# One early load on another queue, other orders of units, and one accumulator bank read by ScalarE instead of VectorE, in a hybrid attention and SwiGLU block

## The chip, the cores and the metric

The kernel runs on one core of one Trainium2 chip. The metric is device time in microseconds. A core has TensorE (PE in the profile; its weight loads are PEld), VectorE (DVE), ScalarE (ACT), GpSimd (POOL) and SyncE (SP). They run apart from each other, each in the order of its own instructions, and wait on semaphores. Weights come from HBM by DMA. In this kernel transfers are issued from SP, which only issues, and from POOL.

## The reference, cut to what matters

One layer on 256 rows of 2048 numbers, all in float32:

```
xn   = rms_norm(x, norm1_g)
proj = xn @ w_in                     # q, k, v and two convolution halves: 5120 columns
mix  = [differential attention ; causal convolution, layer norm, silu]
h    = x + mix @ w_out
hn   = rms_norm(h, norm2_g)
y    = h + (silu(hn @ w_gate) * (hn @ w_up)) @ w_down       # hidden width 5632
```

The change lies in the last line. It is the largest part of the work: w_gate, w_up and w_down are 138 MB of the 197 MB of weights.

## The kernel before, in words

**Precision.** Each float32 operand is split into a rounded part (`hi`) and a rest (`lo`), and a product is three matmuls: hi·hi, lo·hi and hi·lo. ScalarE rounds a weight tile (`whi`, line 334; for pairs `wh`, lines 1028 and 1029). VectorE subtracts to get the rest (`wlo`, line 343; for pairs `wl`, lines 1033 and 1034).

**Units.** The work is a list of chunks, `chunks`, in the order in which TensorE multiplies them. In the feed-forward part a chunk is one letter of an order string:

- `g` or `u`, a *two*: two 128-row weight tiles of one matrix, 512 columns wide, times both halves of the rows; 12 matmuls (lines 1068, 1069 and 1073) and a load of 512 KB. In `fast_block`, `g` stands for the second of a pass's two column blocks (w_gate, or the right block of w_down) and `u` for the first.
- a capital `G` or `U`: the same two, but its rest is made without VectorE. ScalarE writes the negated rounded tile into `wlo` (line 337), and a DMA from POOL's queue adds the raw weights to it (line 338).
- `s`, a *pair*: a product of 2 by 2 blocks (two row halves, two 128-row tiles, two column blocks) with seven products instead of eight, 21 matmuls (lines 1050 to 1052). VectorE makes the sums of weight tiles (`pair_sums`, lines 1022 to 1024). A pair loads 1 MB (`load_pair`, line 1015).

**Passes.** A pass is one order string with its eight accumulator banks, Q1 to Q5, Q6, Q7 and QX. The weights' hidden width is cut into blocks j = 0 to 10 of 512 columns. Block 0 is multiplied plainly (`silu_done`, `up_done`), while `make_forms` prepares the row operand for pairs. Block 1 uses `FIRST`, blocks 2 to 10 `ORDER`. After blocks 3, 7 and 10 come two passes each of w_down, with the orders in `DOWN`. That makes 16 passes with pairs.

**End of a pass.** When the last pair of a pass has been multiplied, `bank_sums` combines the banks on VectorE: line 1148 copies Q1 into `w1`, and lines 1149 to 1154 add Q6, Q7, Q5, Q5, Q2 and Q4 in that order. The twos after the last pair use only Q3 and QX, which `block_done` (line 1168) or `down_done` (line 1202) adds when the pass is over. The next pass takes its banks as they are given back. There are four in the pool `acc` (for Q1, Q6, Q7, Q5) and four in `aux` (for Q2, Q4, Q3, QX, and the transposes `ps_a`, line 891). A pair asks for its banks in the order of `PRODUCTS`: Q6, Q7, Q5, Q1, Q2, Q4, Q3.

**Order.** The schedule is written out by hand: `run_chunks` emits, ahead of each chunk's matmuls, the splits of chunks up to 3 further on, the rounding up to 4, the tiles made by DMA and the sums of pairs up to 5, and the loads up to 9. Code that follows a pass runs as generators, moved on by `resume()` inside the chunks. Raw tiles have four buffers, and SP issues loads in program order: a load that must wait holds up all later loads.

**The early load.** The first pair's weights are loaded by `make_forms`, which calls `load_pair` as soon as the memory pool of the earlier stages is closed. They lie in a tile `wb0` in that memory. SP issues this load.

Of the kernel before, what the change touches and what calls it, by code (L numbers as in the profile page):

```python
# [13 lines left out]
F32 = mybir.dt.float32  # L14
# [5 lines left out]
P = 128  # L20
# [12 lines left out]
N = 512  # L33
# [43 lines left out]

ORDER = "sgGsgGsUUsUu"

FIRST = "gugusgsUsGsU"  # L80

Q1, Q6, Q7, Q5, Q2, Q4, Q3, QX = range(8)

PRODUCTS = ((Q6, 5, 1), (Q7, 6, 2), (Q5, 4, 3), (Q1, 0, 5), (Q2, 1, 6), (Q4, 2, 0), (Q3, 3, 4))

DOWN = (dict(pairs=((1, 0), (1, 1), (2, 0)), order=("gsGgsGgsuUuUu",) * 2),
        dict(pairs=((4, 0), (4, 1), (5, 0)), order=("gsGgsGgsuUuUu",) * 2),
        dict(pairs=((8, 0), (8, 1), (9, 0)), order=("sgsGgsuUu",) * 2))

LOAD_AHEAD, DMA_AHEAD, SUMS_AHEAD, HI_AHEAD, LO_AHEAD = 9, 5, 5, 4, 3  # L90

# [17 lines left out]
def tile_block(  # L109
# [6 lines left out]
    act, dve, pool, pe, sp = nc.scalar, nc.vector, nc.gpsimd, nc.tensor, nc.sync  # L116
# [131 lines left out]
    def start(gen):  # L248
        running.append(gen)

    def resume():
        for g in list(running):
            if next(g, StopIteration) is StopIteration:
                running.remove(g)
# [58 lines left out]
    def weights(parts):  # L313

        n = sum(w for _, _, _, w in parts)
        src = wts[next_weight[0] : next_weight[0] + P * n].rearrange("(p n) -> p n", n=n)
        placed_at.append((next_weight[0], n, parts))
        next_weight[0] += P * n
        return src
# [536 lines left out]
    ffn = {}  # L856
# [39 lines left out]
    def place(g):  # L896

        pairs = DOWN[g]["pairs"]
        at = 7 * len(pairs)
# [53 lines left out]
    def make_forms():  # L953
        fp = ffn["pool"]
        load_pair(chunks[pair_at[0]])
        rep = fp.tile([P, S], F32, tag="sum1", name="rep")
        for m in range(NM):
# [49 lines left out]
    def load_pair(c):  # L1007
        if "b" in c:
            return
        if c is chunks[pair_at[0]]:  # L1010
            c["b"] = ffn["pool"].tile([P, 7, N], F32, tag="wl", name="wb0", bufs=2)[:, :4]
        else:
            c["b"] = early.tile([P, 4, N], F32, tag="wb", name="wb")
        src = weights([(w, k, col, N) for w, col in c["sides"] for k in c["ks"]])
        sp.dma_start(out=c["b"].rearrange("p k n -> p (k n)"), in_=src)

    def pair_sums(c):

# [17 lines left out]
    def sum_bank(c, i):  # L1036
        sums = c["sums"]
        if i not in sums:
            tag, pool_ = ("acc", acc_ps) if i < 4 else ("aux", aux_ps)
            sums[i] = pool_.tile([P, N], F32, tag=tag, name=f"q{i}")  # L1040
        return sums[i]

    def multiply_pair(c):
        while not c["ready"](c):
            resume()
        (fhi, flo), p = c["forms"](), c["p"]
        for n, (q, f, w) in enumerate(PRODUCTS):
            ps = sum_bank(c, q)
            first, last = c["first"].get(q), c["last"].get(q)
            pe.matmul(ps, fhi[:, f, p, :], c["hi"][:, w], start=bool(first), stop=False)  # L1050
            pe.matmul(ps, flo[:, f, p, :], c["hi"][:, w], start=False, stop=False)  # L1051
            pe.matmul(ps, fhi[:, f, p, :], c["lo"][:, w], start=False, stop=bool(last))  # L1052
            if n in (1, 3, 5):
                resume()
        resume()
        if c["done"]:
            start(c["done"](c["sums"]))
# [38 lines left out]
    def fast_block(order, side_u, side_g, pairs, twos, **kw):  # L1096

        units, sums = [], {}
        left = dict(s=list(pairs), g=list(twos), u=list(twos))
        for unit in order:  # L1100
            kind = unit.lower()
            p, ks = left[kind].pop(0)
            c = dict(kind=kind, sums=sums, done=None, first={}, last={}, p=p, ks=ks, by_dma=unit.isupper(), **kw)
            if kind == "s":
                c.update(sides=(side_u, side_g), load=load_pair, round=round_pair, split=split_pair,
                         multiply=multiply_pair, uses=[q for q, _, _ in PRODUCTS])
            else:
                w, col = side_g if kind == "g" else side_u
                c.update(w=w, nk=2, width=N, cols=[(col, N)], load=load_chunk, round=round_chunk, split=split_chunk,
                         multiply=multiply_two, uses=(Q3, QX) if kind == "u" else (Q2, Q4))  # L1110
            units.append(c)
        assert not any(left.values())
        for q in range(8):
            users = [c for c in units if q in c["uses"]]
            users[0]["first"][q] = users[-1]["last"][q] = True
        chunks.extend(units)
        return units

    def gate_up_block(j, order):
        units = fast_block(order, ("w_up", j * N), ("w_gate", j * N), [(k, (k, k + HK)) for k in range(NS)],  # L1120
                           [(None, ks) for ks in TWOS], ready=lambda c: "hi" in forms,
                           forms=lambda: (forms["hi"], forms["lo"]),
                           plain=lambda c: [forms["plain"][k] for k in c["ks"]])
        [c for c in units if c["kind"] == "s"][-1]["done"] = products_done
        units[-1].update(done=lambda sums: block_done(j, sums), prompt=True)

    def down_block(g, n):

        last = g == len(FGROUPS) - 1 and n == D // N - 2
        ks = lambda jt: (jt[0] * (N // P) + 2 * jt[1], jt[0] * (N // P) + 2 * jt[1] + 1)  # L1130
        pairs = DOWN[g]["pairs"]
        twos = [(j, t) for j in range(sum(FGROUPS[:g]), sum(FGROUPS[: g + 1])) for t in range(2) if (j, t) not in pairs]
        units = fast_block(DOWN[g]["order"][n // 2], ("w_down", n * N), ("w_down", (n + 1) * N),
                           [(q, ks(jt)) for q, jt in enumerate(pairs)], [(jt, ks(jt)) for jt in twos],
# [7 lines left out]
    halfway = {}  # L1142

    def bank_sums(q):

        fp = ffn["pool"]
        w1, u2, u3, w4 = (fp.tile([P, N], F32, tag=f"sum{i}", name=f"sum{i}") for i in range(4))
        dve.tensor_copy(w1, q[Q1])  # L1148
        dve.tensor_tensor(u2, q[Q6], w1, ALU.add)
        dve.tensor_tensor(u3, q[Q7], u2, ALU.add)  # L1150
        dve.tensor_tensor(w4, q[Q5], u3, ALU.add)
        dve.tensor_tensor(u2, q[Q5], u2, ALU.add)
        dve.tensor_tensor(w1, q[Q2], w1, ALU.add)
        dve.tensor_tensor(u3, q[Q4], u3, ALU.add)
        halfway.update(g=(w1, u3), u=(u2, w4))

    def products_done(q):
        bank_sums(q)
        for t in halfway["g"]:
            act.activation(t, t, AF.Silu)  # L1160
        yield
# [15 lines left out]
    def down_products(n, q, last):  # L1177
        so_far = None
        if last:
            so_far = ffn["pool"].tile([P, 4, N], F32, tag="wt", name="so_far")[:, :NM]  # L1180
            pool.dma_start(out=so_far, in_=out[:, n * N : (n + 1) * N].rearrange("(m p) n -> p m n", p=P))
        bank_sums(q)
        for m in range(NM):
            add_to_out(m, n + 1, halfway["g"][m])
        yield
        if last:
            for m in range(NM):
                dve.tensor_tensor(halfway["u"][m], halfway["u"][m], so_far[:, m], ALU.add)
        halfway["added"] = True
# [43 lines left out]
    for g, nb in enumerate(FGROUPS):  # L1233
        for j in range(j0, j0 + nb):
            if j:
                gate_up_block(j, FIRST if j == 1 else ORDER)
                continue
# [47 lines left out]
```

## Time and profile before

| | |
|---|---|
| median of 3 runs | 1070.22 us (1069.56 to 1076.16) |
| the profiled execution's own time | 1070.12 us |
| its span, first to last instruction | 1068.3 us |
| granted TensorE clock, mean | 0.997 |
| busy: TensorE, VectorE, ScalarE, GpSimd | 1043.2, 899.5, 653.4, 130.7 us |
| moved by DMA | 245.47 MB, 230 GB/s on average |

A row of the timeline has the start in us from the beginning of the span, the duration, engine, line, operation, the tile written and those read, and in brackets the idle time of the engine before it and what ended that. A row of the waits has who waited for whom, then the total in us, how often, and the longest. A row of the groups has how many instructions, then busy time in us and mean ns of one. A TensorE row's duration overlaps its neighbours, so the pace of matmuls is read from one start to the next. A row of the windows has the busy time and number of instructions of PE, PEld, DVE, ACT and POOL, then the granted clock, the share of time in which the DMA engines were busy, and GB/s.

### The profile page before, as it was taken

How to read it: one execution, taken by the hardware profiler on the slowest of the kernel's cores; microseconds unless marked ns; L12 is line 12 of the kernel's file. 1: busy time of each engine (PE TensorE's matmuls, PEld its weight loads, DVE VectorE, ACT ScalarE, POOL GpSimd, SP SyncE). 2: the span in 40 equal slices, each digit the busy share in tenths (PEclk: the TensorE clock that was granted, in tenths of full speed). 3: DMA queues.
4: the chain of work that ended last, by engine and by line, in shares of the span. 5: the costliest groups of instructions: out<-in, count | busy, mean ns of one | idle time of the engine just before them, and what ended most of it. 6: DMA issues, size and time to landing. Idle time of an engine off the chain costs nothing.

```text
span 1068.3 us, 13248 instructions
## 1 busy us (share of the span) xinstructions
PE 1043.2 (98%) x4780; PEld 860.2 (81%) x4780; DVE 899.5 (84%) x1124; ACT 653.4 (61%) x831; POOL 130.7 (12%) x176
## 2 busy tenths in 40 slices
PE   8999999999999899899999999999999999999998
PEld 7888888877888787687878888878878888888776
DVE  4799988899666389989887789899987897989994
ACT  6544566756656466575665565765764656658551
POOL 0120112200100100010102120100101121001011
PEclk9999999999999999999999999999999999999999
DMA  8656555444446466986969998969878999889774
GB/s 300 206 180 200 189 183 173 158 158 158 158 158 242 171 196 223 291 240 222 320 165 319 269 289 283 290 206 330 235 239 247 262 307 330 239 249 263 242 214 89
DMA packets 62445, 245.47 MB, mean 230 GB/s; under 512 B 6964, under 2 KB 8430, under 8 KB 54956
## 3 DMA queue, kind: packets, MB, share of 16 engines
q1 hardware_dynamic: 48576, 200.56, 52.7%
q0 software_dynamic: 13744, 44.05, 21.6%
q8 instruction: 37, 0.61, 0.2%
q14 instruction: 28, 0.23, 0.1%
q10 hardware_dynamic: 60, 0.03, 0.0%
HBM read 236.22 MB, written 8.39 MB: 229 GB/s over the span
## 4 chain that ended last, share of the span: by engine, by line
PE 51%; DVE 10%; issue 2%; ACT 2%; DMA 1%; DVEq 0%; SPq 0%; ACTq 0%
PE q L1069 9%; PE q L1068 9%; PE q L1073 9%; PE q L1050 7%; PE q L1051 7%; PE q L1052 7%; DVE wl L1034 2%; DVE wt L1022 1%; DVE wlo L343 1%; DVE wt L1023 1%; PE acc L373 1%; PE acc L374 1%; DVE wl L1033 1%; PE ps_a L891 1%; PE acc L379 1%
## 5 line engine op out<-in xcount | busy, mean ns | idle before, releaser
L334 ACT CAST whi<-raw 128x1024 fp32r<-128x1024 f32 (+1 forms) x261 | 268.9, 1046 | 125.6 <-PE q L1069 59.4
L343 DVE TENSOR_TENSOR wlo<-raw,whi 128x1024 fp32r<-128x1024 f32 (+1 forms) x193 | 233.7, 1218 | 74.9 <-ACT whi L334 74.6
L373 PE MATMUL acc<-whi,lhi 128*128 128x512 f32 (+1 forms) x448 | 168.4, 381 | 5.2 <-ACT lhi L240 2.7
L374 PE MATMUL acc<-whi,llo 128*128 128x512 f32 (+1 forms) x448 | 166.6, 377 | 0.5 <-DVE llo L241 0.4
L1029 ACT CAST wh<-wt 128x2048 fp32r<-128x2048 f32 x58 | 110.7, 1909 | 54.0 <-DVE wt L1024 53.8
L1034 DVE TENSOR_TENSOR wl<-wt,wh 128x2048 fp32r<-128x2048 f32 x58 | 132.6, 2287 | 1.6 <-ACT wh L1029 0.9
L1033 DVE TENSOR_TENSOR wl<-wb,wh 128x1536 fp32r<-128x1536 f32 x58 | 101.7, 1753 | 34.9 <-ACT wh L1028 34.9
L1068 PE MATMUL q<-whi,chi 128*128 128x512 f32 x320 | 125.3, 392 | 0.0
L338 POOL DMA_DIRECT2D wlo<-in_wts_dram x68 | 60.8, 894 | 523.0 <-ACT wlo L337 448.0
L1069 PE MATMUL q<-whi,clo 128*128 128x512 f32 x320 | 124.6, 390 | 0.0
L379 PE MATMUL acc<-wlo,lhi 128*128 128x512 f32 (+1 forms) x448 | 114.5, 380 | 1.4 <-DVE wlo L343 1.4
L1050 PE MATMUL q<-wh,fhi 128*128 128x512 f32 x280 | 110.4, 394 | 5.6 <-DVE sum L1148 4.1
L1052 PE MATMUL q<-wl,fhi 128*128 128x512 f32 x280 | 109.8, 392 | 0.0
L1051 PE MATMUL q<-wh,flo 128*128 128x512 f32 x280 | 109.6, 392 | 0.0
L569 DVE SCALAR_TENSOR_TENSOR y<-upad,cw,y 128x256 f32<-128x256 f32 x240 | 103.8, 483 | 4.4 <-ACT y L562 3.9
L373 PEld LDWEIGHTS acc<-whi,lhi 128*128 128x128 f32 x448 | 84.8, 189 | 21.3 <-ACT whi L334 3.3
L374 PEld LDWEIGHTS acc<-whi,llo 128*128 128x128 f32 x448 | 84.8, 189 | 15.8 <-DVE llo L241 0.9
L1028 ACT CAST wh<-wb 128x1536 fp32r<-128x1536 f32 x58 | 85.4, 1472 | 16.7 <-issue 8.5
L379 PEld LDWEIGHTS acc<-wlo,lhi 128*128 128x128 f32 x448 | 79.9, 189 | 16.8 <-DVE wlo L343 2.2
L1073 PE MATMUL q<-wlo,chi 128*128 128x512 f32 x320 | 86.3, 391 | 0.0
L1022 DVE TENSOR_TENSOR wt<-wb 128x1024 f32<-128x1024 f32 x58 | 70.8, 1221 | 3.6 <-DMA wb<-in_wts_dram 3.0
L337 ACT ACTIVATE wlo<-raw 128x1024 fp32r<-128x1024 f32 x68 | 71.8, 1056 | 0.0
(215 smaller groups left out, 1692.0 us busy)
## 6 DMA issues: line engine op xcount, KB each, us to landing
raw<-in_wts_dram SPq DMA_DIRECT2D x259, 512.0 KB, 5.2
wb<-in_wts_dram SPq DMA_DIRECT2D x58, 1024.0 KB, 7.0
wlo<-in_wts_dram POOLq DMA_DIRECT2D x68, 512.0 KB, 8.8
out_dram<-sum POOLq DMA_DIRECT2D x22, 256.0 KB, 7.7
out_dram<-h POOLq DMA_DIRECT2D x8, 256.0 KB, 5.4
h<-in_x_dram SPq DMA_DIRECT2D x6, 256.0 KB, 7.8
h<-in_x_dram SPq DMA_DIRECT2D x4, 128.0 KB, 3.6
raw<-in_wts_dram SPq DMA_DIRECT2D x2, 256.0 KB, 4.4
```

What stands on the lines that cost most here:

```text
L334: act.copy(c["hi"], c["raw"])
L343: dve.tensor_tensor(c["lo"], c["raw"], c["hi"].bitcast(F32), ALU.subtract)
L373: pe.matmul(ps[m], xhi[:, ms], hi[:, j, :], start=c["first"] and j == 0, stop=False)
L374: pe.matmul(ps[m], xlo[:, ms], hi[:, j, :], start=False, stop=False)
L379: pe.matmul(ps[m], xhi[:, ms], lo[:, j, :], start=False, stop=c["last"] and j == nk - 1)
L1034: dve.tensor_tensor(c["lo"][:, :4], c["t"], c["hi"][:, :4].bitcast(F32), ALU.subtract)
L1050: pe.matmul(ps, fhi[:, f, p, :], c["hi"][:, w], start=bool(first), stop=False)
L1051: pe.matmul(ps, flo[:, f, p, :], c["hi"][:, w], start=False, stop=False)
L1052: pe.matmul(ps, fhi[:, f, p, :], c["lo"][:, w], start=False, stop=bool(last))
L1068: pe.matmul(ps, plain[i][0][:, ms], hi[:, i, :], start=i == 0 and bool(c["first"].get(qs[m])), stop=False)
L1069: pe.matmul(ps, plain[i][1][:, ms], hi[:, i, :], start=False, stop=False)
L1073: pe.matmul(sum_bank(c, qs[m]), plain[i][0][:, ms], lo[:, i, :], start=False, stop=i == 1 and bool(c["last"].get(qs[m])))
```

## The change

Three things are edited.

- `load_pair` issues the first pair's load from POOL's queue; all other pairs' loads stay on SP.
- The order strings: in `FIRST` the sixth unit `g` becomes `G`. The four passes of the first two w_down groups begin with the pair and then the `g`, with the same letters otherwise. In the last group's two passes, `sgsGgsuUu` becomes `sGsGgsUUu`, two more capitals each.
- In the last pair of each pass, Q1's product is multiplied first instead of fourth, and directly behind its three matmuls ScalarE is told to copy Q1 into `w1` (tile `sum0`). `bank_sums` takes that tile instead of copying on VectorE.

```diff
-FIRST = "gugusgsUsGsU"
+FIRST = "gugusGsUsGsU"
...
-DOWN = (dict(pairs=((1, 0), (1, 1), (2, 0)), order=("gsGgsGgsuUuUu",) * 2),
-        dict(pairs=((4, 0), (4, 1), (5, 0)), order=("gsGgsGgsuUuUu",) * 2),
-        dict(pairs=((8, 0), (8, 1), (9, 0)), order=("sgsGgsuUu",) * 2))
+DOWN = (dict(pairs=((1, 0), (1, 1), (2, 0)), order=("sgGsgGgsuUuUu",) * 2),
+        dict(pairs=((4, 0), (4, 1), (5, 0)), order=("sgGsgGgsuUuUu",) * 2),
+        dict(pairs=((8, 0), (8, 1), (9, 0)), order=("sGsGgsUUu",) * 2))
...
     def load_pair(c):
         if "b" in c:
             return
+        queue = sp
         if c is chunks[pair_at[0]]:
             c["b"] = ffn["pool"].tile([P, 7, N], F32, tag="wl", name="wb0", bufs=2)[:, :4]
+            queue = pool
...
-        sp.dma_start(out=c["b"].rearrange("p k n -> p (k n)"), in_=src)
+        queue.dma_start(out=c["b"].rearrange("p k n -> p (k n)"), in_=src)
...
-        for n, (q, f, w) in enumerate(PRODUCTS):
+        products = PRODUCTS[3:4] + PRODUCTS[:3] + PRODUCTS[4:] if c["done"] else PRODUCTS
+        for n, (q, f, w) in enumerate(products):
...
+            if n == 0 and c["done"]:
+                halfway["w1"] = ffn["pool"].tile([P, N], F32, tag="sum0", name="sum0")
+                act.copy(halfway["w1"], ps)
...
     def bank_sums(q):
         fp = ffn["pool"]
-        w1, u2, u3, w4 = (fp.tile([P, N], F32, tag=f"sum{i}", name=f"sum{i}") for i in range(4))
-        dve.tensor_copy(w1, q[Q1])
+        w1 = halfway.pop("w1")
+        u2, u3, w4 = (fp.tile([P, N], F32, tag=f"sum{i}", name=f"sum{i}") for i in range(1, 4))
```

## The prediction

> **What bounds the kernel now.** I read the busy times of the page first, then TensorE's waits, then the timeline around each long wait.
>
> ```profile
> span 1068.3 us, 13248 instructions
> PE 1043.2 (98%) x4780; PEld 860.2 (81%) x4780; DVE 899.5 (84%) x1124; ACT 653.4 (61%) x831; POOL 130.7 (12%) x176
> ```
>
> TensorE is the bound, with 25 us in which it is not busy. The change removes no matmul, so all it can give is TensorE's waits in the part that it touches. These are TensorE's waits from 276 us on:
>
> ```profile
> PE q L1050 <- DVE sum L1148: 4.1, 2, 3.8
> PE acc L373 <- ACT whi L334: 2.5, 1, 2.5
> PE ps_a L891 <- DVE a L871: 1.5, 2, 1.2
> PE q L1050 <- DVE sum L1168: 1.3, 1, 1.3
> PE q L1068 <- DVE sum L1153: 1.2, 2, 0.6
> PE ps_a L891 <- DVE llo L924: 1.0, 1, 1.0
> PE q L1050 <- DVE llo L884: 0.8, 1, 0.8
> PE q L1050 <- DVE sum L1152: 0.7, 2, 0.4
> PE q L1069 <- DVE llo L924: 0.7, 1, 0.7
> ```
>
> They sum to 13.8 us. Nearly all name VectorE: it comes late with the end of a pass, while on average it has room. Two of the waits cost more than themselves, as the windows right behind them show (the last three numbers are the granted clock, the share of time in which the DMA engines were busy, and GB/s):
>
> ```profile
> 372.30:375.70 3.40, 3.40 (x9) 2.63 (x8) 3.40 (x4) 2.87 (x3) 0.00 (x0) 0.50 0.92 318
> 451.30:454.80 3.50, 3.50 (x11) 2.65 (x11) 3.50 (x7) 1.88 (x3) 0.00 (x0) 0.58 0.33 129
> ```
>
> After the waits of 2.5 and 3.8 us the clock is near a half for some 3.4 us, so about 1.7 and 1.5 us of work are lost besides. An undisturbed pair gives the pace:
>
> ```profile
> 438.21 0.39 PE L1050 MATMUL q<-wh,fhi 128*128 128x512 f32 x1
> 442.98 0.39 PE L1068 MATMUL q<-whi,chi 128*128 128x512 f32 x1
> ```
>
> That is 4.77 us for 21 matmuls, 0.227 each, 0.68 for a product of three. Each wait also delays the next start by some 0.15 us beyond its row. So the floor, with no wait left, is 1070.1 - 13.8 - 3.2 - 2 = about 1051.
>
> **The early load.** SP's own waits and its timeline, then ACT, PE and DVE at the same place:
>
> ```profile
> SPq L1015 <- DVE ssh L846: 14.0, 1, 14.0
> SPq L1015 <- POOL rstd L218: 2.6, 1, 2.6
> ```
> ```profile
> 364.71 0.33 SPq L1015 DMA_DIRECT2D wb<-in_wts_dram  x1
> 365.09 8.44 SPq L330 DMA_DIRECT2D raw<-in_wts_dram  x5
> ```
> ```profile
> 364.72 0.69 ACT L958 ACTIVATE rep<-ident,rstd 128x128 f32<-128x128 f32 x2 [3.23 <-POOL rstd L218]
> 370.87 1.04 ACT L334 CAST whi<-raw 128x1024 fp32r<-128x1024 f32 x1 [5.46 <-DMA raw<-in_wts_dram]
> ```
> ```profile
> 371.97 0.53 PE L373 MATMUL acc<-whi,lhi 128*128 128x512 f32 x1 [2.50 <-ACT whi L334]
> 376.42 0.39 PE L373 MATMUL acc<-whi,lhi 128*128 128x512 f32 x1
> ```
> ```profile
> 371.95 2.44 DVE L343 TENSOR_TENSOR wlo<-raw,whi 128x1024 fp32r<-128x1024 f32 x2 [8.88 <-ACT whi L334]
> ```
>
> The first pair's load sits 16.6 us at the head of SP until the second norm is done, and the raw loads behind it all leave at once when it goes. ScalarE, TensorE and VectorE then wait for the first of them. On POOL the load waits for nothing that POOL has not just computed itself, and SP's raw loads go as buffers come free. So ScalarE rounds that tile right after `rep`, from 365.4 to 366.4, and VectorE starts at 366.45 instead of 371.95: **VectorE is 5.5 us earlier**. TensorE loses the wait (2.5) and the half clock (376.42 - 371.97 = 4.45 for a chunk of 12 matmuls that takes 2.72, so 1.7): **TensorE is 4.2 us earlier**. VectorE's chain to 404 us (forms, splits, then `a`, line 871) moves with its start, so the waits of 1.5 us on line 871 shrink until TensorE too is 5.5 earlier. The 0.8 us on line 884 stays, both being shifted alike. On POOL the load costs an issue, and what follows there has room:
>
> ```profile
> 415.40 0.95 POOL L338 DMA_DIRECT2D wlo<-in_wts_dram  x1 [50.72 <-ACT wlo L337]
> ```
>
> 512 KB took 0.95 us to issue; for 1 MB I bound it by 0.95 and 1.9, and POOL is idle for 50 us around it. Nobody needs the tile before 400 us, so even a slow landing is covered.
>
> The Trainium skill (Trainium Kernel Development and Optimization, Key Constraints) says that transfers from SP, ACT and POOL run on the same 16 DMA engines and that issuing from several only saves issue time. By that rule this part would bring next to nothing, and it is the first rival below; the two wait rows of SP speak against it here, as what is saved is a wait in SP's order.
>
> **The sixth unit of FIRST and the copy.** Now the start of the second pass with pairs:
>
> ```profile
> 417.43 1.22 DVE L343 TENSOR_TENSOR wlo<-raw,whi 128x1024 fp32r<-128x1024 f32 x1
> ...
> 448.83 0.68 DVE L1148 COPY sum<-q 128x512 f32<-128x512 f32 x1
> 449.55 0.69 DVE L1149 TENSOR_TENSOR sum<-q,sum 128x512 f32<-128x512 f32 x1
> 451.61 0.68 DVE L1152 TENSOR_TENSOR sum<-q,sum 128x512 f32<-128x512 f32 x1
> ```
> ```profile
> 449.66 0.47 PE L1050 MATMUL q<-wh,fhi 128*128 128x512 f32 x1 [3.80 <-DVE sum L1148]
> 456.17 0.39 PE L1068 MATMUL q<-whi,chi 128*128 128x512 f32 x1
> ```
> ```profile
> 496.35 0.50 PE L1050 MATMUL q<-wh,fhi 128*128 128x512 f32 x1 [0.35 <-DVE sum L1152]
> ```
>
> The first product of a pass takes the bank that line 1148 gives back, the fourth the one of line 1152: banks go round in the order of release, so the second waits for line 1149. Therefore the early copy frees only the **first** product, and the second is next to be late. Line 1149 ended at 450.24. It moves by 5.5 (above), by 1.1 (the split at 417.43, which goes to ScalarE and a DMA) and by 0.7 (line 1148), to 442.9. TensorE, 5.5 earlier, begins the pair at 445.86 - 5.5 = 440.4, wants its second product at 441.0, and waits 1.9 us. The fourth wants line 1152, at 452.3 - 7.3 = 445.0, and waits 0.7 more. The pair ends at 440.4 + 4.8 + 1.9 + 0.7 = 447.7 instead of 456.2: **8.5 us saved up to here**. I take no half clock behind 1.9 us, the smallest gap with one being 2.5; if it comes, it costs 1.7.
>
> ScalarE's price:
>
> ```profile
> L689 ACT COPY kT<-ps_qk 128x512 f32<-128x512 f32 x4 | 2.4, 591 | 8.1 <-PE ps_qk L688 8.1
> L337 ACT ACTIVATE wlo<-raw 128x1024 fp32r<-128x1024 f32 x68 | 71.8, 1056 | 0.0
> ```
>
> 16 copies of 0.59 us (the same shape out of a bank) and five negations of 1.06 make 15 us on an engine that is idle for 415. VectorE loses 16 times 0.69 and five times 1.22, 17 us. What the copy can hold up on ScalarE is the rounding of a chunk five further on, more than 10 us ahead; in the passes of w_gate and w_up the silu behind it waits for line 1153 anyway. So I cost it at nothing; without that cover it is 0.6 us a pass.
>
> **The later passes.** The wait on line 1148 of 0.3 us and those on line 1152 (0.7) go, as the sums come 0.7 earlier; I keep 0.2, so 0.8 saved. The two of 0.6 us on line 1153 are at the start of w_down passes, where `g` wants Q2's bank first; with a pair first that bank is wanted 2.7 us later, and 1.2 is saved. The passes of w_up and w_gate begin with a pair now and show what this may cost: the 0.4 at most on line 1152. In the last group:
>
> ```profile
> 1002.90 1.28 DVE L1168 TENSOR_TENSOR sum<-q,sum 128x512 f32<-128x512 f32 x2
> ...
> 1012.89 0.68 DVE L924 TENSOR_TENSOR llo<-ps_a,lhi 128x512 fp32r<-128x512 f32 x1
> ```
> ```profile
> 1013.63 0.66 PE L891 MATMUL ps_a<-ident,sum 128*128 128x128 f32 x4 [1.03 <-DVE llo L924]
> ```
>
> VectorE comes to line 1168 with 0.7 (copy) and 1.1 (the split of the second unit, now `G`) less before it, so the 1.3 us on it goes. Line 924 is 1.8 earlier, but TensorE 1.3, so 0.5 of that 1.0 goes. Before the next line 924 one more split falls away (`u` to `U`), and its 0.7 goes. That is 2.5 us, and 0.15 beyond the row for each of seven waits that end adds about 1. Five more tiles by DMA are 2.6 MB on 245.
>
> The sum is 8.5 + 0.8 + 1.2 + 2.5, rounded up by 0.6 of that 1 us: 13.6 us. From the profiled execution's 1070.1 (its span and 1.8 around it; the median is 1070.2) this gives **1056.5 us**.
>
> **The rivals.**
>
> *SP's order isn't what was late*, or POOL issues the load no earlier for the others (the skill's rule, above). The 2.5 us wait, the half clock and the 1.5 us on line 871 stay; VectorE gains only the 1.8 us of removed work before the second pass. Its line 1149 ends at 448.4, the pair's six other products and 0.7 of waits end at 453.2, and 3.0 instead of 8.5 is saved: 1062. For it: a burst of five loads would have to land anyway. Against: 8.88 us of VectorE idle.
>
> *The transfers become the bound* between 400 and 450 us:
>
> ```profile
> 430.00:440.00 10.00, 10.00 (x45) 8.28 (x45) 8.55 (x8) 6.67 (x5) 0.86 (x1) 1.00 1.01 333
> ```
>
> Here the DMA engines are full. If pairs arrive no earlier than now, VectorE's 5.5 us are eaten before the second pass, and the time is again 1062, though the wait at 372 is gone. Against it: the chain VectorE, buffer, load moves as a whole, and the tile added by DMA is issued before this window.
>
> *The copy comes late*, ScalarE being in order behind a rounding that waits for VectorE's own sums of pairs. Then line 1149 waits for it and VectorE's 0.7 us a pass isn't gained where it counts (the second pass, 0.7; the third, 0.5; the last group, 0.7): 1058.5.
>
> *Everything goes*: the sums of the second pass come before TensorE wants them: 1051.
>
> *Slower: a pass that begins with a pair makes VectorE late.* Sums and splits of the pair stand in VectorE's queue before the adds of lines 1168 and 1202, and the seventh product needs a bank that those give back. The only w_down pass that begins right after a w_gate pass with a pair now is the last group's, and it has waits of 1.3, 1.0 and 0.7 us where the others have 0.6. If the four changed passes each pay 3.0 us, the last group gains nothing and the 1.2 isn't won, the balance is 12.0 - 8.5 - 0.8 = +2.7: 1073, and up to 1.7 more for each gap that halves the clock. It decides when the adds end more than 4.1 us (18 matmuls) after the pass begins. Against it: w_down has six splits in 13 units besides three pairs, less than VectorE carries in w_gate passes, which begin with a pair without such waits.
>
> **How the numbers follow.** Chances: forecast 0.52, everything goes 0.12, copy late 0.08, SP's order 0.09, transfers 0.13, slower 0.06. Within 1% (10.7 us, what a measurement here can tell from no change) lie SP's order, transfers and most of the slower case. That makes 0.72 faster, 0.26 within, 0.02 slower. The range runs from the floor of 1051 over the two cases at 1062 with 2 us for their bounds, to 1064; the slower case is left out.
>
> **What would show it.** In the profile after: no wait of SP on line 1015 for `ssh`; no wait of TensorE near 370 us and no half clock there; one wait of about 2 us at the start of the second pass, ended by line 1149's add and not by the copy; no waits at the start of w_down passes; VectorE some 17 us less busy, ScalarE 15 more. Wrong would be: waits of TensorE at the seventh product of w_down passes, TensorE waiting for `wlo` that a DMA makes, or ScalarE idle before the copy with roundings late behind it.

## The result, and the profile after

| | before | after |
|---|---|---|
| median of 6 runs each | 1070.34 us | 1058.76 us |
| lowest to highest | 1069.56 to 1076.16 | 1058.64 to 1059.67 |
| the profiled execution's own time | 1070.12 us | 1059.67 us |

The changed kernel takes 0.9883 of the time, with a 95% interval of 0.9861 to 0.9905. That is 11.6 us less, where 13.6 were forecast. The profiled execution after is itself 0.9 us above its median, and loses more than that ahead of the change: line 962's transpose, which nothing in the change touches, starts at 366.30 instead of 365.17 us. The traces show why. Behind a wait of TensorE near 15 us the clock is at a half for 3.41 us in this execution, and not in the profiled one before. Of the fourteen traces of this document seven have that half clock, with and without each part of the change, and in them line 962 starts at 365.98 to 367.40 us; in the other seven it starts at 364.99 to 365.35. So it belongs to the execution and not to the kernel. It costs some 1.4 us: the 300 matmuls behind that wait take 48.7 us instead of 47.3. Savings below are therefore counted from that transpose on: the start of the same matmul in both traces, each less the start of its own line 962. The medians of the experiments can't be cleared of it, so differences between them of about 1.5 us or less decide little.

In the kernel after, most of the lines that matter have moved: the pair's load is line 1017, its sums 1024 to 1026, `wh` 1030 and 1031, `wl` 1035 and 1036, its matmuls 1053 to 1055, the twos 1074, 1075 and 1079, the new copy 1058, the adds of `bank_sums` 1155 to 1160 (before 1149 to 1154), `block_done` 1174, `down_done` 1208. Lines below 1000 are unchanged.

The span and the busy times of the page after:

```profile
span 1057.9 us, 13283 instructions
PE 1038.6 (98%) x4780; PEld 859.5 (81%) x4780; DVE 883.5 (84%) x1103; ACT 667.0 (63%) x852; POOL 136.5 (13%) x182
```

VectorE is 16.0 us less busy and ScalarE 13.6 more (17 and 15 forecast). TensorE's waits after, from 270 us on:

```profile
PE ps_a L891 <- DVE a L871: 1.5, 2, 1.2
PE q L1053 <- DVE sum L1155: 1.4, 2, 0.9
PE ps_a L891 <- DVE llo L924: 1.0, 1, 1.0
PE q L1053 <- DVE sum L1174: 0.9, 1, 0.9
PE q L1053 <- DVE sum L1208: 0.9, 1, 0.9
PE q L1053 <- DVE sum L1158: 0.9, 2, 0.4
PE q L1053 <- DVE llo L884: 0.8, 1, 0.8
PE ps_r L962 <- ACT rep L958: 0.3, 1, 0.3
```

They sum to 7.7 us; by the same window it was 14.1 before. The 2.5 us on line 334, the 3.8 on the copy and those at the entries into w_down are gone. One is new: 0.9 us on line 1208.

Where the load was moved, first SP's own waits after between 300 and 400 us, then GpSimd's and VectorE's timeline:

```profile
...
SPq L330 <- DVE ssh L846: 3.4, 1, 3.4
```
```profile
366.37 0.61 POOL L1017 DMA_DIRECT2D wb<-in_wts_dram  x1 [0.56 <-DMA raw<-in_wts_dram]
```
```profile
367.51 2.44 DVE L343 TENSOR_TENSOR wlo<-raw,whi 128x1024 fp32r<-128x1024 f32 x2 [3.31 <-ACT whi L334]
```

SP no longer waits for the second norm with a load of a pair (a raw load still waits 3.4 us for it). VectorE starts 1.21 us behind line 962's transpose; before it was 371.95 - 365.17 = 6.78. It is 5.57 us earlier, with 5.5 forecast. The start of the second pass with pairs (TensorE's timeline after), and the windows at the two places where the clock had been near a half:

```profile
442.30 0.39 PE L1053 MATMUL q<-wh,fhi 128*128 128x512 f32 x1
...
444.02 0.50 PE L1053 MATMUL q<-wh,fhi 128*128 128x512 f32 x1 [0.89 <-DVE sum L1155]
...
446.21 0.50 PE L1053 MATMUL q<-wh,fhi 128*128 128x512 f32 x1 [0.43 <-DVE sum L1158]
...
449.08 0.39 PE L1074 MATMUL q<-whi,chi 128*128 128x512 f32 x1
```
```profile
372.30:375.70 3.40, 3.40 (x17) 2.81 (x16) 3.40 (x4) 0.00 (x0) 0.00 (x0) 1.00 0.96 360
444.00:447.40 3.40, 2.95 (x11) 1.99 (x12) 3.22 (x6) 1.92 (x3) 0.00 (x0) 1.00 0.86 248
```

The first product waits for nothing, the second for the first add and the fourth for line 1158, as the prediction named them; the granted clock is 1.00 in both windows.

This is what had been saved at the same matmul, in us (the start in the kernel before names the place; e6 and e9 are experiments that follow):

| up to | forecast | after | e6 | e9 |
|---|---|---|---|---|
| 379, behind the wait on line 334 | 4.2 | 4.4 | 4.4 | 0.0 |
| 459, behind the pair of the second pass | 8.5 | 8.2 | 9.1 | 2.7 |
| 504, behind the pair of the third pass | 9.0 | 7.8 | 10.4 | 3.6 |
| 965, at the last group | 10.5 | 11.4 | 13.0 | 6.0 |
| the last matmul | 13.6 | 11.6 | 16.8 | 8.6 |

So the shortfall has two places: the third pass, where 0.4 us are lost, and the last group, which gives 0.2 us of 2.5. Between them 3.6 us were gained where 1.5 were forecast: 2.5 where waits are gone as forecast (the entries into w_down, and line 1152 near 707 us), and the rest at three places that stay open. What VectorE stood for at the two places that failed, by its timeline after:

```profile
470.78 1.76 DVE L1035 TENSOR_TENSOR wl<-wb,wh 128x1536 fp32r<-128x1536 f32 x1 [3.43 <-ACT wh L1030]
...
977.65 1.76 DVE L1035 TENSOR_TENSOR wl<-wb,wh 128x1536 fp32r<-128x1536 f32 x1 [1.43 <-ACT wh L1030]
...
1011.64 1.76 DVE L1035 TENSOR_TENSOR wl<-wb,wh 128x1536 fp32r<-128x1536 f32 x1 [3.77 <-ACT wh L1030]
```

And what ScalarE did then:

```profile
468.32 1.05 ACT L337 ACTIVATE wlo<-raw 128x1024 fp32r<-128x1024 f32 x1
469.28 1.46 ACT L1030 CAST wh<-wb 128x1536 fp32r<-128x1536 f32 x1
...
974.24 1.06 ACT L334 CAST whi<-raw 128x1024 fp32r<-128x1024 f32 x1 [3.43 <-PE q L1075]
975.20 1.06 ACT L337 ACTIVATE wlo<-raw 128x1024 fp32r<-128x1024 f32 x1
976.16 1.47 ACT L1030 CAST wh<-wb 128x1536 fp32r<-128x1536 f32 x1
...
1008.23 1.05 ACT L334 CAST whi<-raw 128x1024 fp32r<-128x1024 f32 x1 [1.62 <-PE q L1075]
1009.18 1.06 ACT L337 ACTIVATE wlo<-raw 128x1024 fp32r<-128x1024 f32 x1
1010.14 1.46 ACT L1030 CAST wh<-wb 128x1536 fp32r<-128x1536 f32 x1
```

Each time the rounding and negation of a capital (lines 334 and 337), five chunks ahead, stand in front of the pair's `wh`, for which VectorE waits. In the last group it is worse: the capital's `whi` needs a buffer that TensorE is still reading, so ScalarE stops for 3.4 us with `wh` behind it, and for 1.6 us the second time. This reading gave the main theory for the experiments: **VectorE is late because ScalarE is, and ScalarE is late because of the order in which its work is written out.** The rival was the prediction's own: VectorE simply has too much to do ahead of these adds. The Trainium skill (PSUM — Partial Sum Buffer, Engine vs sequencer instructions) says that the queues of ScalarE and VectorE are strictly first in, first out; the rows above agree, as `wh` starts only behind the blocked `whi` (974.24 us) and its negation (975.20 us), at 976.16.

### The profile page after: what moved, and what is told of

Same layout as the page of the kernel before. It is cut to its first block, busy times and chain, and to the rows that moved or that the text cites. A ratio compares the mean times of both kernels' runs of the same rounds, so it can differ in the third digit from the quotient of the medians.

```text
span 1057.9 us, 13283 instructions
## 1 busy us (share of the span) xinstructions
PE 1038.6 (98%) x4780; PEld 859.5 (81%) x4780; DVE 883.5 (84%) x1103; ACT 667.0 (63%) x852; POOL 136.5 (13%) x182
## 4 chain that ended last, share of the span: by engine, by line
PE 56%; DVE 7%; issue 2%; ACT 1%; POOL 0%; DVEq 0%; ACTq 0%; POOLq 0%
PE q L1074 10%; PE q L1075 10%; PE q L1079 10%; PE q L1053 8%; PE q L1054 8%; PE q L1055 8%; DVE wl L1036 1%; DVE wlo L343 1%; DVE wl L1035 1%; DVE wt L1024 1%; PE ps_a L891 1%; PE acc L379 1%; PE acc L374 1%; PE acc L373 1%; DVE wt L1025 0%
## 5 line engine op out<-in xcount | busy, mean ns | idle before, releaser
L343 DVE TENSOR_TENSOR wlo<-raw,whi 128x1024 fp32r<-128x1024 f32 (+1 forms) x188 | 228.0, 1220 | 84.8 <-ACT whi L334 84.6
L338 POOL DMA_DIRECT2D wlo<-in_wts_dram x73 | 63.9, 875 | 522.1 <-ACT wlo L337 487.6
L1035 DVE TENSOR_TENSOR wl<-wb,wh 128x1536 fp32r<-128x1536 f32 x58 | 101.7, 1754 | 29.7 <-ACT wh L1030 29.7
L337 ACT ACTIVATE wlo<-raw 128x1024 fp32r<-128x1024 f32 x73 | 77.1, 1056 | 0.0
```

Of the source, the lines that this page charges most:

```text
L343: dve.tensor_tensor(c["lo"], c["raw"], c["hi"].bitcast(F32), ALU.subtract)
```

## The experiments

Each batch ran beside the kernel before on its own chip, whose median was 1071.05 us for e1 to e4, 1070.53 for e5 to e8 and 1070.74 for e9 to e12. Ratios are to that.

**e1 to e3: each part alone**, put into the kernel before.

e1 has only the load on GpSimd's queue:

```diff
+        queue = sp
         if c is chunks[pair_at[0]]:
+            queue = pool
...
-        sp.dma_start(
+        queue.dma_start(
```

> The kernel before with only the first pair's load moved to GpSimd's queue. Theory (the load blocks SP's order, and VectorE's chain starts with the raw load behind it): no wait of TensorE near 372 us, VectorE's chain about 4.5 us earlier up to 404 us, and the wait on line 1148 at the second pass about as long as now; 1065 us, 5 us saved. Rival (a load on another queue only saves issue time): the wait near 372 us stays; 1070 us.

1066.37 us, ratio 0.9962 [0.9948, 0.9975], 4.7 us less. TensorE's waits of e1 at the second and third pass (4.2 and 0.7 us) and a later one:

```profile
PE q L1052 <- DVE sum L1150: 5.2, 3, 4.2
```

The 2.5 us at 372 and its half clock are gone, but what VectorE and TensorE gain together leaves the gap between them at the second pass as it was (4.2 us on the copy, which is line 1150 here, and a half clock behind it). That refutes the first rival of the prediction: issuing from another queue did save more than issue time, as what it took away was a wait of SP's.

e2 has only the copy on ScalarE, with Q1 multiplied first in the last pair.

> The kernel before with only ScalarE's early copy of Q1 and Q1's product first in the last pair. Theory (the copy frees only the first product's bank; the second waits for line 1149): at the second pass TensorE waits some 3 us at the second product instead of 3.8 at the first, and elsewhere waits of 0.3 to 0.7 shrink; 1068 us, 2 us saved. Rival (the copy itself takes the long wait away): no wait over 1 us at the second pass; 1064 us.

1067.30 us, 0.9962 [0.9947, 0.9977], 3.8 us less, where 2 were expected: by the trace 1.0 us is saved up to the third pass, and the rest at later passes. TensorE's waits of e2:

```profile
PE q L1051 <- DVE sum L1153: 3.0, 1, 3.0
```

The first product waits no more, and the second waits 3.0 us for the first add (line 1153 here), with a half clock behind it (0.62 granted from 450.90 to 454.30 us): the banks do go round in the order of release.

e3 has only the order strings.

> The kernel before with only the new order strings. Theory: the wait at the second pass shrinks by the split that goes (1.1 us), the two waits of 0.6 us at the start of w_down passes go, and the last group gains little (under 0.5 us), because its second unit as a capital makes ScalarE wait for a buffer; 1067 us. Rival (the prediction's account of the last group, 2.5 us there): 1065 us.

1066.09 us, 0.9951 [0.9936, 0.9966], 5.0 us less. TensorE's waits of e3 (lines as in the kernel before):

```profile
PE q L1050 <- DVE sum L1148: 2.9, 2, 1.6
...
PE q L1050 <- DVE sum L1168: 1.5, 1, 1.5
PE q L1050 <- DVE sum L1202: 1.5, 1, 1.5
```

`FIRST` alone brings the second pass's wait from 3.8 to 1.6 us, and with it the half clock goes; at the third pass the wait on line 1148 grows from 0.3 to 1.3. In the last group the new capitals make line 1168 slightly worse (1.3 before) and bring a new wait of 1.5 us on line 1202; by the trace that group loses 1.0 us. The medians of the three parts alone sum to 13.4 us. By the traces, counted behind line 962, they save 4.0, 3.9 and 4.2 us, 12.0 in all, and the whole change 11.6: the parts nearly add up.

**e4 and e8: the last group's capitals.** e4 is the changed kernel with that group's order as before:

```diff
-        dict(pairs=((8, 0), (8, 1), (9, 0)), order=("sGsGgsUUu",) * 2))
+        dict(pairs=((8, 0), (8, 1), (9, 0)), order=("sgsGgsuUu",) * 2))
```

> The changed kernel with the last group's order as before (sgsGgsuUu). Theory (in the last group what two capitals give is lost again, ScalarE being held by a buffer that TensorE still reads, so that VectorE idles 1.4 and 3.8 us): 1059 us, within 0.5 us of the changed kernel; the wait of 0.9 us on line 1208 is absent, and those on line 924 are both there. Rival (the two capitals saved the 2.5 us of the prediction): 1061 us.

1057.96 us, 0.9872 [0.9856, 0.9889]. TensorE's waits of e4:

```profile
PE ps_a L891 <- DVE llo L924: 1.0, 1, 1.0
...
PE q L1075 <- DVE llo L924: 0.7, 1, 0.7
PE q L1053 <- DVE sum L1174: 0.4, 1, 0.4
```

No wait on line 1208, and 0.4 instead of 0.9 on line 1174, without the capitals: they paid for what they took off VectorE with what they put ahead of it on ScalarE. VectorE's own list agrees: from 960 to 1025 us it stands 5.2 us for `wh` in the changed kernel, and not at all in e4.

e8 keeps the later of the two new capitals (`sgsGgsUUu`).

> The changed kernel with only the later one of the two new capitals in the last group's passes (sgsGgsUUu instead of sGsGgsUUu). Theory (the early capital is what blocks ScalarE, the late one is what removed the wait of 0.7 us on the second line 924): no wait on line 1208, about 0.4 us on line 1174, 1.0 on the first line 924 and none on the second; 0.7 us below the last group as before, 1057.2 on the scale of the changed kernel's 1058.8. Rival (both waits on the sums come from the late capital): line 1208 keeps 0.9 us and the time stays at 1058.8.

1056.87 us, 0.9876 [0.9861, 0.9890]. TensorE's waits of e8 have no row for line 1208, only the first 1.0 us on line 924, and at line 1174 the 0.4 us that e4 has.

So the early capital is the harmful one. In their medians e4, e8 and the changed kernel aren't apart (the intervals overlap). Counted at the same matmuls, from 965 us of the kernel before to the last one, they are: the last group gives 0.2 us in the changed kernel, -0.1 to 0.2 in e5, e7 and e12, which share its orders, 0.9 in e4 and 1.9 in e8.

**e7: the second pass with one more capital** (the changed kernel with the fifth unit of block 2 as `G`: `sgGsGGsUUsUu`; the expectation's words speak of two, only this letter differs).

> The changed kernel with two more lower-case gate twos of the second pass (block 2) made without VectorE: its fifth unit becomes a capital and one later up two too (sgGsGGsUUsUu instead of sgGsgGsUUsUu). Theory (the waits of 0.54 and 0.43 us at the start of the third pass come from VectorE being late with the whole second pass, its lead having been used up): one split of 1.2 us less on VectorE, both waits gone, 1.0 to 1.2 us less, 1057.7. Rival (the order of banks sets those waits, or ScalarE and not VectorE is late): they stay within 0.2 us, and the extra negation makes the time the same or 0.3 us worse.

1057.53 us, 0.9884 [0.9867, 0.9900]. The wait of 0.54 us on the first add of the third pass is gone, one of 0.3 on line 1160 (1158 in the changed kernel) stays. Behind the second pass's pair 9.3 us had been saved (8.2 in the changed kernel; the difference is there already at line 871, ahead of the edit), behind the third's 9.9 (7.8): 1.1 us more comes from the third pass. So VectorE's load does count there. This run can't say whether VectorE is late by its own work or by ScalarE's.

**e6: the swap.** One swap in `run_chunks` of the changed kernel: the usual roundings are written out ahead of those for the DMAs.

```diff
-                until("dma", round_of, t + 1 + DMA_AHEAD, lambda c: c["by_dma"])
                 until("round", round_of, t + 1 + (HI_AHEAD if t >= first else LO_AHEAD))
+                until("dma", round_of, t + 1 + DMA_AHEAD, lambda c: c["by_dma"])
```

> The changed kernel with one swap in the emitted order: ahead of each chunk ScalarE's usual roundings come before the tiles that it prepares for the DMAs, in all passes. Theory (in the last group VectorE stands because ScalarE is stuck in the rounding of a capital whose buffer is still read, with the pair's rounding behind it): ScalarE's waits of 3.4 us at 974 and 1.3 and 1.6 us at 1005 to 1008 no longer hold up VectorE's line 1035, the waits on lines 1174 (0.9) and 1208 (0.9) fall below 0.4 each, about 1.3 us less, 1057.5. Rival (VectorE simply has too much before those adds): both waits stay within 0.2 us, 1058.8.

**1054.08 us** (1052.19 to 1054.59), 0.9847 [0.9832, 0.9862]; its slowest run is below the fastest of e5, e7 and e8 (1056.34) on the same chip. All of TensorE's waits of e6 from 270 us on:

```profile
PE ps_a L891 <- DVE a L871: 1.3, 2, 0.9
PE q L1053 <- DVE llo L884: 0.8, 1, 0.8
PE q L1079 <- ACT whi L334: 0.7, 1, 0.7
PE q L1053 <- DVE sum L1158: 0.4, 1, 0.4
PE ps_r L962 <- ACT rep L958: 0.3, 1, 0.3
```

Not two but all waits of the last group are gone, line 924's too, and the two of the third pass. No work was taken off any engine (VectorE 882.7 us busy, ScalarE 667.7). VectorE's stand for `wh` ahead of the third pass fell from 3.4 to 1.5 us, and what it stands for `wh` from 960 to 1025 us from 5.2 to 1.7. New is 0.7 us for a `whi` near 517 us. The theory holds, and it was sized too small: 4 to 5 us instead of 1.3. The swap also exchanges the buffers that two neighbouring `whi` tiles take; no run separates that from the order.

**e9: the same swap in the kernel before**, without any part of the change.

> The kernel before with only the swap of the emitted order (ScalarE's usual roundings ahead of the tiles that it prepares for the DMAs). Theory (VectorE's lateness in the kernel before was in part ScalarE's order, as it too has VectorE standing 3.4 us for wh at 477 us): the waits at the start of the third pass (0.3 and 0.35 us) and the 0.6 at 537 and 789 us go or halve, the 3.8 us at 449.7 fall by up to 1.2, and the time is 2 to 3 us below the kernel before. Rival (only the capitals that the change adds make that order harmful): the same as the kernel before within 0.6 us, with its waits as they were.

1062.15 us, 0.9918 [0.9902, 0.9935], **8.6 us less** than before; 2 to 3 were expected. TensorE's waits of e9 (the first four rows) show what is left:

```profile
PE acc L373 <- ACT whi L334: 2.5, 1, 2.5
PE ps_a L891 <- DVE a L871: 1.6, 2, 1.2
PE q L1073 <- DMA wlo<-in_wts_dram: 1.6, 3, 0.8
PE q L1050 <- DVE sum L1148: 0.9, 1, 0.9
```

3.8 us became 0.9 at the second pass, without the half clock, and the waits on lines 1153 and 1168 are gone. The swap has a price: tiles that a DMA adds to arrive later, 1.6 us in three waits on them. Now the view that the prediction leaves out, VectorE's own waits from 404 to 1040 us, first in the kernel before, then in e9:

```profile
DVE wl L1033 <- ACT wh L1028: 34.9, 13, 3.8
DVE wlo L343 <- ACT whi L334: 22.6, 15, 4.4
```
```profile
DVE wl L1033 <- ACT wh L1028: 9.7, 10, 1.5
```

In the kernel before VectorE stood 35 us for `wh`, of which the swap takes away 25. VectorE has as much work as before (899.0 us busy, 899.5 before), and its idle time shrinks only by what the span does, some 8 us: it now stands elsewhere (28.3 us in four waits ahead of splits, for which the trace names no releaser), and TensorE waits less for it. TensorE's waits named VectorE; VectorE's named ScalarE; and ScalarE's order was the larger cause. VectorE's own work counts beside it: in the kernel before it stands 0.5 us in all from 960 to 1030 us and is late all the same, e7 gained 1.1 us by one split less, and in e2 the copy gave 0.8 us in the last group.

**e10: the swap with the last group's order as before.**

> The changed kernel with the swap and with the last group's order as before (no new capitals there). Theory (once ScalarE no longer blocks, the capitals do what they were costed at, by taking splits off VectorE): the waits of 1.0 and 0.7 us on line 924 are back and 0.3 us or so on line 1174, the time is 1.5 to 2 us above the swap with capitals, 1055.8. Rival (the swap alone takes away the last group's waits and the capitals are not needed): no waits there, 1054.1 as with them.

1055.10 us, 0.9854 [0.9837, 0.9871], not apart from e6. TensorE's only wait of e10 in the last group:

```profile
PE q L1075 <- DVE llo L924: 0.3, 1, 0.3
```

Of the waits on line 924 only 0.3 is back, not 1.7. So the rival is nearly right. Counted at the same matmuls, the last group gives 3.2 us in e10 and 3.8 in e6: once ScalarE's order is mended, the two capitals are worth some 0.6 us.

**e5 and e11: the first load later.** In the changed kernel the first pair's load was under way together with raw loads. Here a GpSimd operation on the first half of `clo` stands ahead of it:

```diff
-        load_pair(chunks[pair_at[0]])
...
+            if i == 0:
+                pool.tensor_tensor(late, clo[:, 0, :1].bitcast(F32), clo[:, 0, :1].bitcast(F32), ALU.mult)
+                load_pair(chunks[pair_at[0]])
```

> The changed kernel with the first pair's load held on GpSimd until half of the rest of the normed rows has been written (near 379 us), so that it no longer lands among the raw loads of 366 to 376 us. Theory (the load's 1 MB collides with those loads and takes a good part of VectorE's lead): ScalarE's wait for raw at 376 us, 5.2 us, falls to 3 or less, VectorE has more of its 5.5 us left at 401 us, the two waits on line 871 fall from 1.5 us to below 0.6, and the second pass's waits fall with them; the time falls by 0.8 to 1.5 us, to about 1057.5. Rival (the five raw loads alone need that long, the 1 MB adds nothing): waits as in the changed kernel, 1058.8 within 0.4.

1058.26 us, 0.9888 [0.9873, 0.9902]: no difference in the medians. ScalarE's timeline in the changed kernel and in e5, at the same rounding:

```profile
376.00 1.05 ACT L334 CAST whi<-raw 128x1024 fp32r<-128x1024 f32 x1 [5.22 <-DMA raw<-in_wts_dram]
```
```profile
371.22 1.06 ACT L335 CAST whi<-raw 128x1024 fp32r<-128x1024 f32 x1 [1.66 <-PE acc L375]
```

The collision is real: the first raw load issued behind the pair's took 7.1 us to land after, 3.4 in e5, and ScalarE no longer waits for it. The waits on line 871 fell to 0.3 us, and TensorE came 1.1 us earlier. But they were as small in e7 and e10, which issue the load early, and between 0.6 and 1.5 in the other profiles that do. In these eight profiles that raw load landed after 5.5 to 7.1 us, and the later it landed, the longer the waits on line 871. So what the collision costs varies from run to run, and the medians don't show it.

e11 has the swap and the later load.

> The changed kernel with the swap and with the first pair's load held until near 379 us. Theory (the two gains lie in different places and add): the waits on line 871 are 0.3 us instead of 1.3, none on lines 1155, 1158, 1174, 924, 1208 above 0.5 us, 1053.2. Rival (with the swap VectorE has enough lead, and what the later load gives is lost at the next wait): 1054.1.

1054.24 us, 0.9841 [0.9826, 0.9856]. By its trace 17.9 us were saved behind line 962 against 16.8 in e6, as the theory had it, but the medians are the same, so it is not shown that this is worth anything in time.

**e12: the copy made twice.** The changed kernel with `act.copy` issued twice in a row.

> The changed kernel with the copy of the first bank made twice in each pass, 16 more copies of 0.57 us on ScalarE. Theory (the copy costs nothing on ScalarE, as the roundings behind it are far ahead of their use): 1058.8 within 0.5, waits as in the changed kernel. Rival (ScalarE's time counts where VectorE stands behind it, in the second and third pass and in the last group): those waits grow by 0.3 to 0.6 us each, 1060 or more; if it counted in every pass, 1068.

1058.26 us, 0.9881 [0.9866, 0.9897], with ScalarE 9.3 us busier. TensorE's waits of e12 on the adds are those of the changed kernel:

```profile
PE q L1053 <- DVE sum L1156: 1.4, 2, 0.9
...
PE q L1053 <- DVE sum L1209: 0.9, 1, 0.9
```

The copy costs nothing on ScalarE that shows here, not even doubled. At this place ScalarE's amount of work makes nothing late; with e6 this points to what stands in front of what.

## Why the prediction was right, and where it was not

The measured 1058.8 us is 2.2 above the forecast of 1056.5 and inside the range; 1.2% faster is what the likeliest case said. Step by step:

- **The early load** was right: the wait, the half clock (4.4 us for 4.2) and VectorE's 5.5 us. That the waits on line 871 would shrink until TensorE is 5.5 earlier too failed in the profiled execution (4.5) and came true in e7 (5.6). The load's issue, bounded by 0.95 and 1.9 us, took 0.61.
- **FIRST and the copy** came to 8.2 us for 8.5. The waits were smaller than forecast (0.9 and 0.4 for 1.9 and 0.7), as TensorE came 0.8 us later than forecast; VectorE's first add ended within 0.1 us of its forecast. That the second product is next to be late is shown by e2 as well. That no half clock follows came true, but behind 0.9 us; behind the 1.9 us of the forecast it would have been luck, as the last section shows.
- **ScalarE's copy at nothing** was right, as far as e12 can show. The same sentence costed the negations by the 415 us in which ScalarE is idle. That step failed: busy time isn't the measure, as they stand in the queue ahead of roundings that VectorE waits for.
- **The later passes.** The waits at the entries into w_down and the one on line 1152 near 707 us went as forecast; up to the last group 11.4 us were saved for 10.5, of which some 1.2 came from places that the forecast doesn't name. The waits at the start of the third pass did not go but grew from 0.65 to 0.97 us. TensorE reached it earlier by more than VectorE did; VectorE still stood 3.4 us for `wh` on the way, as it had in the kernel before. e6 takes these waits away.
- **The last group** is the step that failed: 0.2 us instead of 2.5. "VectorE comes to line 1168 with 0.7 and 1.1 less before it" left out that it then stands 1.4 and 3.8 us for ScalarE, which holds the new capitals ahead of the pair. Of the 1.3 us on line 1168 (1174 after) only 0.4 went, the first wait on line 924 stayed whole, the second went as forecast, and the new wait on line 1208 took 1.1 us back. e4, e8 and e6 show this from three sides.
- **The rivals.** That SP's order isn't late is refuted by e1. The wait of the slower rival did appear at its place, the seventh product of a w_down pass (in the last group's two passes: 0.9 us on line 1174, where the kernel before has 1.3, and 0.9 on line 1208), but not in the passes of the first two groups, which begin with a pair now, and its cause isn't the pair in front: e6 keeps that order and has no such wait. "Everything goes" (1051) was not reached; the swap comes nearest to it, with 1054.1.

The larger error doesn't show in the number. The prediction said that VectorE comes late with the end of a pass and costed what is taken off VectorE. In fact a swap that takes nothing off VectorE gives the kernel before 8.6 us, most of what the change gives. So the change seems to have worked in part by giving VectorE enough lead to stand and wait; after it VectorE still stands 29.7 us for `wh` between 404 and 1040 us. e6, the change with the swap, is the fastest of all together with e11: 16.5 us below the kernel before, and 4 to 5 below the change.

Open is why some 0.3 us each were gained near 551, 803 and 958 us, where TensorE stands 0.06 us at most in the kernel before, and why the raw load in the collision behind 366 us lands now sooner and now later.

## What to carry to other kernels

When the bound engine's waits name another engine, read that engine's own waits before costing what to take off it; the cause may be one engine further, in an order and not in an amount of work. On an engine that works in order, what is prepared furthest ahead is not free: if it can block on a buffer, write it out behind what is needed first. Changes that shorten the late engine's work hide such a cause, and the gain then stops where the queue is blocked again.

## What the hardware showed that was not expected

The clock fell behind shorter pauses than expected, and the length of a pause alone doesn't decide whether it falls. Near 15 us all fourteen traces have a wait of TensorE for the tile that line 240 writes, of 1.5 to 2.6 us. Here it is in the changed kernel and in e4, each with a window behind it:

```profile
14.74 0.38 PE L373 MATMUL acc<-whi,lhi 128*128 128x256 f32 x1 [1.97 <-ACT lhi L240]
15.10:18.50 3.40, 3.27 (x16) 3.24 (x16) 2.51 (x5) 2.96 (x7) 0.00 (x0) 0.50 1.02 339
```
```profile
15.14 0.38 PE L373 MATMUL acc<-whi,lhi 128*128 128x256 f32 x1 [2.63 <-ACT lhi L240]
15.10:18.50 3.40, 3.22 (x25) 3.03 (x26) 2.89 (x5) 3.37 (x9) 0.00 (x0) 1.00 1.00 309
```

The shorter wait has the half clock and the longer one has none. At this place it came with waits of 1.88 us (e1) to 2.62 us (e11), and it stayed away with others of 2.07 (the kernel before), 2.61 (e9) and 2.63 us. Later in the traces all waits of 2.4 us and more had it (2.4 to 2.5 at 372 in the kernel before, e2, e3 and e9, and 3.0, 3.8 and 4.2 at the second pass), and those of 1.6 us and below had none, as behind the 1.6 us in e3:

```profile
447.60:451.00 3.40, 3.04 (x13) 2.06 (x14) 3.33 (x6) 1.33 (x2) 0.00 (x0) 1.00 0.80 237
```

Each fall behind a wait lasted 3.41 us (6.83 in e11). So in these traces a wait of 1.9 to 2.6 us may or may not cost a half clock. The Trainium skill (TensorE: Matmul & The Clock Gate, What's actually happening) puts the fall after at least one idle window of about 3.4 us; here falls came behind waits from 1.88 us on.
